# Sums of squares of the MLA latents moved behind the split transposes, and the first heads' weight splits moved to VectorE

## The chip, the cores and the metric

The kernel runs on one core of a Trainium2 chip. The metric is device time in microseconds (us). Engines are named as in the profile: PE is TensorE (PEld its weight loads), DVE is VectorE, ACT is ScalarE, POOL is GpSimd, SP is SyncE, whose queue issues the weight transfers.

## The reference, cut to what matters

Two blocks of two layers each run over 256 tokens of width 1024 in float32. The change lies in the first layer's mixer, an attention with low-rank latents (MLA):

```
proj = h @ w_in                    # 1024 -> 384 + 256 + 64
c_q, c_kv, k_pe = split(proj)
q  = rms_norm(c_q,  q_a_norm)  @ w_uq     # 8 heads x (128 + 64)
kv = rms_norm(c_kv, kv_a_norm) @ w_ukv    # 8 heads x (128 + 128)
k_pe = rope(rms_norm(k_pe, k_rope_norm))
```

Each `rms_norm` needs, per token, the sum of squares of its part: 384 columns of `c_q`, 256 of `c_kv`, 64 of `k_pe`. The attention of the eight heads, the output projection, an MLP and three more layers follow.

## The kernel before, in words

**Split products.** A float32 product is made of three matmuls on split operands: each operand is written as a rounded high part and a low part (the rest), and `mm3` (L174 to L176) issues high x high, high x low and low x high. So every weight and every activation is split once. `load_w` (L150 to L171) does it for weights: SP issues the transfer into a tile `raw` (L163), ACT writes `whi` (L166), and a second engine writes `wlo = raw - whi` (L167). That engine is VectorE unless the caller names others; `(G,)` names GpSimd. The tiles raw, whi and wlo are rings of four buffers each, 1024 columns wide: a transfer waits until the split four tiles earlier has been read, a split until the matmuls that read the tile four earlier are done. `evac_split` (L252 to L261) does it for activations that PE has transposed into PSUM: ACT writes the high part (L259), VectorE the low part (L260).

**The first mixer, `mla` (L482).** The input projection fills four PSUM banks, two for each of the two token tiles t: `a[t][0]` with the 384 columns of c_q, `a[t][1]` with the 256 of c_kv and the 64 of k_pe. These four are the whole ring `acc`. VectorE copies them to SBUF (`ct` and `kp`, L516 to L518). VectorE then takes the six sums of squares from these copies, with a multiply whose accumulator gives the sum (L519 to L522). PE transposes the latents, five blocks of 128 columns for both token tiles (L527), into the ring `aux` of four PSUM banks, and `evac_split` empties them into `cT`. The statistics `vv` (L535) and `rr` (a reciprocal square root by Newton steps on VectorE, L185 to L190) follow from the sums; the rotated `k_pe` follows from `rr`.

**Head pairs, `heads(hp)` (L561).** For each of four pairs of heads: the q weights (3 x 384 columns, in tiles of 768 and 384), nine `mm3` products' worth of matmuls for each token tile into `aq[t]`, then, for hp 0 and 2, the kv weights (two tiles of 1024 columns), and `ak[t]`. `aq[0]`, `aq[1]`, `ak[0]`, `ak[1]` take over the banks of `a[0][0]`, `a[0][1]`, `a[1][0]`, `a[1][1]`. ACT copies the results out (L579 to L582) and takes sums of squares; VectorE makes the head norms (L590, L595, L185 to L190, L600); PE transposes (L608); `attention(hp)` follows. For hp 0 alone both `load_w` calls name GpSimd.

**The order of the work.** The text gives priorities only. A planner lays the instructions of each engine in a queue by its own estimate of when each is ready, and the chip works off each queue in that order. So the second Newton step of `rr` stands, in the queue of VectorE, around the splits of the weights of pair 1. The planner runs anew for a changed text.

Of the kernel before, what the change touches and what calls it, by code (L numbers as in the profile page):

```python
# [13 lines left out]
AF = mybir.ActivationFunctionType  # L14
ALU = mybir.AluOpType
# [4 lines left out]
P = 128  # L20
S = 256
NT = 2
# [88 lines left out]
def kernel(ctx: ExitStack, tc: tile.TileContext, I: dict, out: bass.AP, small_at: dict):  # L111
    nc = tc.nc
    V, A, G, T = nc.vector, nc.scalar, nc.gpsimd, nc.tensor
# [10 lines left out]
    def slot(i, shape, dt=F32):  # L124

        return big.tile(shape, dt, tag=f"s{i}", name=f"s{i}")

    def w2k(shape, dt=F32):
        return wk.tile(shape, dt, tag="w2k", name="w2k", bufs=7)

    def w1k(shape, dt=F32):
        return wk.tile(shape, dt, tag="w1k", name="w1k", bufs=3)

    def acc_tile():
        return ps.tile([P, 512], F32, tag="acc", name="acc")

    def aux_tile():
        return ps.tile([P, 512], F32, tag="aux", name="aux")

    @contextmanager  # L140
    def queued(after):

        with ExitStack() as es:
            for i in after or ():
                es.enter_context(tc.issue_after(i))
            yield
# [3 lines left out]
    def load_w(src, a, b, engines=None, into=None, after=None):  # L150

        m = max(1, 1024 // b)
        parts = []
        for a0 in range(0, a, m):
            k = min(m, a - a0)
            raw = ring.tile([P, 1024], F32, tag="raw", name="raw")
            if into is None:
                hi = ring.tile([P, 1024], F32R, tag="whi", name="whi")
                lo = ring.tile([P, 1024], F32R, tag="wlo", name="wlo")
            else:  # L160
                hi, lo = (t[:, a0 * b:(a0 + k) * b] for t in into)
            rs = raw[:, :k * b]
            nc.sync.dma_start(rs.rearrange("p (a b) -> p a b", a=k), src[:, a0:a0 + k])  # L163
            e = V if engines is None else engines[a0 // m % len(engines)]
            with queued(after):
                i = A.activation(hi[:, :k * b], rs, AF.Copy)  # L166
                j = e.tensor_tensor(lo[:, :k * b], rs, hi[:, :k * b].bitcast(F32), op=ALU.subtract)  # L167
            split[:] = [i.ins, j.ins]
            for i in range(k):
                parts.append((hi[:, i * b:(i + 1) * b], lo[:, i * b:(i + 1) * b]))  # L170
        return parts  # L171
# [81 lines left out]
    def evac_split(hi, lo, p, g=None):  # L253

        if g is None:
            i = A.activation(hi, p, AF.Copy)
            j = V.tensor_tensor(lo, p, hi.bitcast(F32), op=ALU.subtract)
        else:
            i = A.activation(hi, p, AF.Copy, scale=g)  # L259
            j = V.scalar_tensor_tensor(lo, p, g, hi.bitcast(F32), op0=ALU.mult, op1=ALU.subtract)  # L260
        return i.ins, j.ins  # L261

    def pair_tile(i, n):
        return slot(i, [P, n, S], F32R), slot(i + 1, [P, n, S], F32R)
# [217 lines left out]
    def mla():  # L482
        hT = pair_tile(1, KD)
        w = wview("mla_w_in", 0)
        a = [[acc_tile() for _ in range(2)] for _ in range(NT)]
        grp = ((0, Q_RANK), (Q_RANK, KV_RANK + ROPE))
        behind = []
        for c in range(4):
            nc.sync.dma_start(xT0[:, 2 * c:2 * c + 2], I["xT"][:, 2 * c:2 * c + 2])
            for k in (2 * c, 2 * c + 1):  # L490
                hi = A.activation(hT[0][:, k], xT0[:, k], AF.Copy, scale=gain("attn_norm", k))
                lo = V.scalar_tensor_tensor(hT[1][:, k], xT0[:, k], gain("attn_norm", k), hT[0][:, k].bitcast(F32),
                                            op0=ALU.mult, op1=ALU.subtract)
            wc = load_w(w[:, 2 * c:2 * c + 2, :], 2, 704)
# [17 lines left out]
        ct = slot(13, [P, NT, 640])  # L512
        kp = w1k([P, NT, 1, ROPE])
        ss = st.tile([P, NT, 3], F32, tag="ss3", name="ss3")
        for t in range(NT):
            V.tensor_copy(ct[:, t, 0:384], a[t][0][:, 0:384])  # L516
            V.tensor_copy(ct[:, t, 384:640], a[t][1][:, 0:256])
            V.tensor_copy(kp[:, t, 0], a[t][1][:, 256:320])  # L518
        for t in range(NT):  # L519
            for j, (src, n) in enumerate(((ct[:, t, 0:384], 384), (ct[:, t, 384:640], 256), (kp[:, t, 0], 64))):  # L520
                jk = w2k([P, 512])
                V.scalar_tensor_tensor(jk[:, :n], src, 1.0, src, op0=ALU.mult, op1=ALU.mult, accum_out=ss[:, t, j:j + 1])  # L522
        cT = pair_tile(11, 5)
        for k in range(5):
            p = aux_tile()
            for t in range(NT):
                T.transpose(p[:, t * P:(t + 1) * P], ct[:, t, k * P:(k + 1) * P], ident)  # L527
            g = gain("mla_q_a_norm", k) if k < 3 else gain("mla_kv_a_norm", k - 3)
            evac_split(cT[0][:, k], cT[1][:, k], p[:, 0:256], g)
        vv = st.tile([P, NT, 3], F32, tag="vv", name="vv")  # L530
        rr = st.tile([P, NT, 3], F32, tag="rr", name="rr")
        ee = st.tile([P, NT], F32, tag="ee", name="ee")
# [20 lines left out]
        wq = wview("mla_w_uq", 0)  # L553
        wkv = wview("mla_w_ukv", 0)
# [4 lines left out]
        wkv_c, roped = [], []  # L559

        def heads(hp):  # L561
            wc = load_w(wq[:, :, hp * 384:(hp + 1) * 384], 3, 384, (G,) if hp == 0 else None)
            aq = [acc_tile() for _ in range(NT)]
            for t in range(NT):
                for k in range(3):
                    mm3(aq[t][:, :384], sl(cT, slice(None), k, slice(t * P, (t + 1) * P)), wc[k],
                        k == 0, k == 2)
            if hp % 2 == 0:
                wkv_c[:] = load_w(wkv[:, :, hp * 512:hp * 512 + 1024], 2, 1024, (G,) if hp == 0 else None)
            ak = [acc_tile() for _ in range(NT)]  # L570
            for t in range(NT):
                for k in range(2):
                    mm3(ak[t], sl(cT, slice(None), 3 + k, slice(t * P, (t + 1) * P)),
                        sl(wkv_c[k], slice(None), slice((hp % 2) * 512, (hp % 2) * 512 + 512)), k == 0, k == 1)
            s6 = st.tile([P, NT, 3, 2], F32, tag="s6", name="s6")
            r6 = st.tile([P, NT, 3, 2], F32, tag="r6", name="r6")
            raw = slot(9 + hp % 2, [P, NT, 2, 320])
            for t in range(NT):
                A.activation(raw[:, t, :, 0:192], aq[t][:, :384].rearrange("p (h d) -> p h d", h=2), AF.Copy)  # L579
                k3 = ak[t].rearrange("p (h d) -> p h d", h=2)  # L580
                A.activation(raw[:, t, :, 192:320], k3[:, :, 0:128], AF.Copy)
                A.activation(vt[:, t, 2 * hp:2 * hp + 2, :], k3[:, :, 128:256], AF.Copy, scale=rr[:, t, 1:2])  # L582
            for t in range(NT):
                for j in range(2):
                    for i, (src, n) in enumerate(((aq[t][:, 192 * j:192 * j + 128], P), (aq[t][:, 192 * j + 128:192 * j + 192], ROPE),
                                                  (ak[t][:, 256 * j:256 * j + 128], P))):
                        sq = w1k([P, P])
                        if i == 2:
                            rw = raw[:, t, j, (0, 128, 192)[i]:(0, 128, 192)[i] + n]
                            V.scalar_tensor_tensor(sq[:, 0:n], rw, 1.0, rw, op0=ALU.mult, op1=ALU.mult,  # L590
                                                   accum_out=s6[:, t, i, j:j + 1])
                        else:
                            A.activation(sq[:, 0:n], src, AF.Square, accum_out=s6[:, t, i, j:j + 1])
            f3 = lambda ap: ap.rearrange("p a b c -> p (a b c)")
            V.tensor_tensor(s6, s6, eq, op=ALU.add)  # L595
            rsqrt(f3(r6), f3(s6), 12)
            qn = w2k([P, NT, 2, P])
            kn = w2k([P, NT, 2, P])
            for dst, c0, i in ((qn, 0, 0), (kn, 192, 2)):
                V.tensor_tensor(dst, raw[:, :, :, c0:c0 + P], r6[:, :, i, :, None].to_broadcast([P, NT, 2, P]), op=ALU.mult)  # L600
            qr = w1k([P, NT, 2, ROPE])
            roped[:] = [rope_apply(G, qr, raw[:, :, :, 128:192], tabs["q"], 2)]
            V.tensor_tensor(qr, qr, r6[:, :, 1, :, None].to_broadcast([P, NT, 2, ROPE]), op=ALU.mult)
            for src, dst, g in ((qn, qT, gs[:, 0:1]), (kn, kT, gs[:, 3:4])):
                p = aux_tile()
                for j in range(2):
                    for t in range(NT):
                        T.transpose(p[:, j * S + t * P:j * S + (t + 1) * P], src[:, t, j], ident)  # L608
                A.activation(dst[:, 2 * hp:2 * hp + 2, :], p.rearrange("p (a b) -> p a b", a=2), AF.Copy, scale=g)
            p = aux_tile()  # L610
            for t in range(NT):
                T.transpose(p[:, t * P:(t + 1) * P], qr[:, t].rearrange("p a b -> p (a b)"), ident)
            V.tensor_copy(peT[:, hp, :], p[:, 0:256])
# [674 lines left out]
    with queued(mla()):  # L1288
        rel_bias_mask()
# [30 lines left out]
```

## Time and profile before

| | us |
|---|---|
| median of 3 runs | 964.49 |
| lowest, highest | 960.13, 966.01 |
| the profiled execution | 965.93 |
| its span, first to last instruction | 964.1 |
| mean granted clock of TensorE | 0.979 |

The span is what the rows below cover, counted from the first instruction; 1.8 us of the execution lie around it. An idle time of an engine is shown in brackets ahead of the instruction that ended it, with what released it. Instructions of one engine overlap a little at their ends: the distance from start to start is what one costs its queue.

### The profile page before, as it was taken

To read this page: it belongs to the slowest core of one execution; us is meant where nothing else is said; L and a number is where in the kernel's file an instruction comes from. 1 tells how busy PE (TensorE), PEld (TensorE's weight loads), DVE (VectorE), ACT (ScalarE), POOL (GpSimd) and SP (SyncE) were. 2 spreads that over 40 slices of the span, in tenths; PEclk is the share of its full clock that TensorE was granted. 3 is DMA by queue.
4 is the path that set the end of the run, shared out by engine and by line. 5 is a ranking of instruction groups with operands and counts; after the bars stand their busy time and mean duration, and the time that the engine had idled before them with its cause. 6 is when DMAs were issued, how large, how long until landed. Compare 5 with 4: busy or idle time off the path is not lost. (4 is left out here: it accounts for less than half of the span.)

```text
span 964.1 us, 14699 instructions
## 1 busy us (share of the span) xinstructions
PE 905.0 (94%) x5474; PEld 789.9 (82%) x5474; DVE 635.4 (66%) x1335; ACT 522.7 (54%) x967; POOL 151.1 (16%) x194
## 2 busy tenths in 40 slices
PE   8799889999999999999999999998995998998995
PEld 8676589989998878778999999888994986887784
DVE  6897376655556666757554555678983688757775
ACT  6576354644556556646534454478653136754652
POOL 1421122222222300022000000010387000000000
PEclk9799999999999999999999999999997999999998
DMA  8345247677767864436666566354843115445431
GB/s 292 115 146 186 66 131 220 192 198 214 205 197 209 166 196 151 154 109 198 196 195 198 175 195 183 105 166 140 215 149 98 45 41 181 135 170 174 133 109 67
DMA packets 97304, 154.62 MB, mean 160 GB/s; under 512 B 10840, under 2 KB 65920, under 8 KB 96976
## 3 DMA queue, kind: packets, MB, share of 16 engines
q1 hardware_dynamic: 87072, 141.53, 46.9%
q0 software_dynamic: 10016, 12.11, 6.0%
q8 instruction: 43, 0.70, 0.3%
q14 instruction: 29, 0.24, 0.1%
q10 hardware_dynamic: 144, 0.03, 0.0%
HBM read 147.84 MB, written 5.78 MB: 159 GB/s over the span
## 5 line engine op out<-in xcount | busy, mean ns | idle before, releaser
L167 DVE TENSOR_TENSOR wlo<-raw,whi 128x1024 fp32r<-128x1024 f32 (+3 forms) x194 | 236.7, 1223 | 201.9 <-ACT whi L166 200.6
L166 ACT ACTIVATE whi<-raw 128x1024 fp32r<-128x1024 f32 (+3 forms) x202 | 206.0, 1025 | 217.0 <-DMA raw<-in_mlp_w_in_dram 137.6
L174 PE MATMUL acc<-whi,s 128*128 128x512 f32 (+2 forms) x408 | 162.1, 401 | 3.5 <-ACT whi L166 2.6
L175 PE MATMUL acc<-wlo,s 128*128 128x512 f32 (+2 forms) x408 | 160.4, 394 | 0.5 <-DVE wlo L167 0.5
L176 PE MATMUL acc<-whi,s 128*128 128x512 f32 (+2 forms) x408 | 158.9, 391 | 0.0
L176 PE MATMUL aux<-s,wlo 128*128 128x256 f32 (+2 forms) x528 | 149.5, 283 | 3.1 <-DVE wlo L167 3.1
L174 PE MATMUL aux<-s,whi 128*128 128x256 f32 (+2 forms) x528 | 149.4, 283 | 2.3 <-DVE s L260 2.3
L175 PE MATMUL aux<-s,whi 128*128 128x256 f32 (+2 forms) x528 | 149.3, 283 | 0.0
L174 PEld LDWEIGHTS aux<-s,whi 128*128 128x128 f32 (+2 forms) x528 | 99.6, 189 | 4.6 <-DVE s L260 2.8
L176 PEld LDWEIGHTS aux<-s,wlo 128*128 128x128 f32 (+2 forms) x528 | 99.6, 189 | 3.9 <-DVE wlo L167 3.6
L174 PE MATMUL acc<-s,w2k 128*128 128x512 f32 x256 | 100.1, 391 | 1.7 <-ACT w2k L676 1.7
L176 PE MATMUL acc<-s,w2k 128*128 128x512 f32 x256 | 100.2, 391 | 1.1 <-DVE w2k L677 1.1
L175 PEld LDWEIGHTS aux<-s,whi 128*128 128x128 f32 (+2 forms) x528 | 99.6, 189 | 1.6
L175 PE MATMUL acc<-s,w2k 128*128 128x512 f32 x256 | 100.0, 391 | 0.0
L174 PEld LDWEIGHTS acc<-whi,s 128*128 128x128 f32 x408 | 77.6, 191 | 20.6 <-ACT whi L166 3.1
L176 PEld LDWEIGHTS acc<-whi,s 128*128 128x128 f32 x408 | 78.6, 193 | 14.0 <-DVE s L1278 0.3
L175 PEld LDWEIGHTS acc<-wlo,s 128*128 128x128 f32 x408 | 78.2, 192 | 13.2 <-DVE wlo L167 1.3
L167 DVE TENSOR_TENSOR s<-raw,s 128x1024 fp32r<-128x1024 f32 x64 | 75.7, 1219 | 5.3 <-ACT s L166 5.3
L176 PE MATMUL acc<-s,wlo 128*128 128x256 f32 x256 | 73.4, 288 | 6.2 <-DVE wlo L167 6.2
L175 PE MATMUL acc<-s,whi 128*128 128x256 f32 x256 | 73.7, 288 | 0.5 <-DVE s L260 0.2
L174 PE MATMUL acc<-s,whi 128*128 128x256 f32 x256 | 73.7, 288 | 0.4 <-ACT s L259 0.2
L166 ACT ACTIVATE s<-raw 128x1024 fp32r<-128x1024 f32 x68 | 68.3, 1048 | 7.2 <-DMA raw<-in_mlp_w_out_dram 6.0
(357 smaller groups left out, 1486.2 us busy)
## 6 DMA issues: line engine op xcount, KB each, us to landing
raw<-in_mlp_w_in_dram SPq DMA_DIRECT2D x64, 512.0 KB, 5.3
raw<-in_mlp_w_out_dram SPq DMA_DIRECT2D x64, 512.0 KB, 3.9
raw<-in_gdn_w_in_dram SPq DMA_DIRECT2D x32, 512.0 KB, 4.4
raw<-in_moba_w_qkv_dram SPq DMA_DIRECT2D x24, 512.0 KB, 4.4
raw<-in_fox_w_in_dram SPq DMA_DIRECT2D x16, 512.0 KB, 4.9
raw<-in_kv_w_dram SPq DMA_DIRECT2D x16, 512.0 KB, 3.9
raw<-in_mla_w_o_dram SPq DMA_DIRECT2D x8, 512.0 KB, 3.9
bias_d<-s POOLq DMA_DIRECT2D x64, 64.0 KB, 4.5
```

The costliest lines, as they stand in the source:

```text
L166: i = A.activation(hi[:, :k * b], rs, AF.Copy)
L167: j = e.tensor_tensor(lo[:, :k * b], rs, hi[:, :k * b].bitcast(F32), op=ALU.subtract)
L174: T.matmul(o, lhsT=l[0], rhs=r[0], start=start, stop=False)
L175: T.matmul(o, lhsT=l[0], rhs=r[1], start=False, stop=False)
L176: T.matmul(o, lhsT=l[1], rhs=r[0], start=False, stop=stop)
```

## The change

The sums of squares move, in the text, behind the transposes and their splits. The two sums of c_q (384 columns) go to ScalarE, from the copy in SBUF. The four sums of c_kv and k_pe stay on VectorE, but one of the two factors is read from PSUM, from `a[t][1]`, and the other from the copy. The two `load_w` calls of the first head pair no longer name GpSimd, so their four splits run on VectorE.

```diff
-        for t in range(NT):
-            for j, (src, n) in enumerate(((ct[:, t, 0:384], 384), (ct[:, t, 384:640], 256), (kp[:, t, 0], 64))):
-                jk = w2k([P, 512])
-                V.scalar_tensor_tensor(jk[:, :n], src, 1.0, src, op0=ALU.mult, op1=ALU.mult, accum_out=ss[:, t, j:j + 1])
         cT = pair_tile(11, 5)
         for k in range(5):
...
             evac_split(cT[0][:, k], cT[1][:, k], p[:, 0:256], g)
+        for t in range(NT):
+            jk = w2k([P, 512])
+            A.activation(jk[:, :384], ct[:, t, 0:384], AF.Square, accum_out=ss[:, t, 0:1])
+        for t in range(NT):
+            for j, (c0, n, src) in enumerate(((0, 256, ct[:, t, 384:640]), (256, 64, kp[:, t, 0]))):
+                jk = w2k([P, 512])
+                V.scalar_tensor_tensor(jk[:, :n], a[t][1][:, c0:c0 + n], 1.0, src, op0=ALU.mult, op1=ALU.mult,
+                                       accum_out=ss[:, t, 1 + j:2 + j])
...
-            wc = load_w(wq[:, :, hp * 384:(hp + 1) * 384], 3, 384, (G,) if hp == 0 else None)
+            wc = load_w(wq[:, :, hp * 384:(hp + 1) * 384], 3, 384)
...
-                wkv_c[:] = load_w(wkv[:, :, hp * 512:hp * 512 + 1024], 2, 1024, (G,) if hp == 0 else None)
+                wkv_c[:] = load_w(wkv[:, :, hp * 512:hp * 512 + 1024], 2, 1024)
```

## Rows read from the trace of the kernel before

**Rows 1.** The page, part 1: PE's busy time and share.

```profile
PE 905.0 (94%) x5474; PEld 789.9 (82%) x5474; DVE 635.4 (66%) x1335; ACT 522.7 (54%) x967; POOL 151.1 (16%) x194
```

**Rows 2.** Busy time by stretch (start:end and length first; PEclk is the granted clock).

```profile
core 0: us, PE busy (x) PEld busy (x) DVE busy (x) ACT busy (x) POOL busy (x), PEclk, DMA share, GB/s
...
28.00:34.00 6.00, 0.69 (x2) 0.38 (x3) 6.00 (x10) 1.17 (x2) 4.96 (x2) 0.59 0.53 159
34.00:39.00 5.00, 5.00 (x17) 5.00 (x17) 2.94 (x19) 1.81 (x3) 0.00 (x0) 0.50 0.15 39
...
50.00:92.00 42.00, 41.10 (x207) 30.57 (x208) 37.38 (x120) 28.73 (x92) 9.63 (x13) 1.00 0.58 182
```

**Rows 3.** Waits of PE from 22 to 50 us: total, times, longest.

```profile
PE aux L527 <- DVE s L260: 5.0, 1, 5.0
PE acc L174 <- ACT whi L166: 1.0, 1, 1.0
```

**Rows 4.** VectorE in order of time: start, duration, line, operation, [idle before].

```profile
25.61 0.21 DVE L518 COPY w1k<-acc 128x64 f32<-128x64 f32 x1
25.75 1.06 DVE L522 SCALAR_TENSOR_TENSOR w2k<-s 128x384 f32<-128x384 f32 x1
...
27.88 0.22 DVE L522 SCALAR_TENSOR_TENSOR w2k<-w1k 128x64 f32<-128x64 f32 x1
...
28.51 2.56 DVE L522 SCALAR_TENSOR_TENSOR w2k<-s 128x256 f32<-128x256 f32 x1
...
31.00 2.35 DVE L522 SCALAR_TENSOR_TENSOR w2k<-w1k 128x64 f32<-128x64 f32 x1
...
33.27 2.25 DVE L260 SCALAR_TENSOR_TENSOR s<-aux,gains,s 128x256 fp32r<-128x256 f32 x5
35.44 0.29 DVE L535 SCALAR_TENSOR_TENSOR vv<-ss,ee 128x2 f32<-128x2 f32 x3
```

**Rows 5.** GpSimd in order of time: the first head pair's splits.

```profile
24.57 3.10 POOL L167 TENSOR_TENSOR wlo<-raw,whi 128x768 fp32r<-128x768 f32 x2 [1.44 <-ACT whi L166]
28.30 4.96 POOL L167 TENSOR_TENSOR wlo<-raw,whi 128x1024 fp32r<-128x1024 f32 x2 [0.63 <-ACT whi L166]
```

**Rows 6.** PE in order of time, around its wait and behind it.

```profile
26.73 0.34 PE L174 MATMUL acc<-whi,s 128*128 128x384 f32 x1
26.90 0.33 PE L175 MATMUL acc<-wlo,s 128*128 128x384 f32 x1
...
33.80 0.69 PE L527 MATMUL aux<-gains,s 128*128 128x128 f32 x2 [5.03 <-DVE s L260]
34.15 0.67 PE L176 MATMUL acc<-whi,s 128*128 128x384 f32 x1
...
38.77 0.63 PE L175 MATMUL acc<-wlo,s 128*128 128x512 f32 x1
...
41.58 0.41 PE L174 MATMUL acc<-whi,s 128*128 128x384 f32 x1
```

**Rows 7.** VectorE behind the statistics: splits for pair 1, pair 0's norm, pair 2's split.

```profile
38.98 0.96 DVE L167 TENSOR_TENSOR wlo<-raw,whi 128x768 fp32r<-128x768 f32 x1 [1.78 <-ACT whi L166]
...
39.95 0.56 DVE L167 TENSOR_TENSOR wlo<-raw,whi 128x384 fp32r<-128x384 f32 x1
...
49.49 1.29 DVE L600 TENSOR_TENSOR w2k<-s,r 128x512 f32<-128x512 f32 x2
...
51.25 1.22 DVE L167 TENSOR_TENSOR wlo<-raw,whi 128x1024 fp32r<-128x1024 f32 x1
```

**Rows 8.** ScalarE in order of time: a sum of squares, the latents' high parts, weight splits.

```profile
21.27 0.62 ACT L240 ACTIVATE w2k<-x 128x512 f32<-128x512 f32 x1
...
25.71 1.57 ACT L259 ACTIVATE s<-aux,gains 128x256 fp32r<-128x256 f32 x4 [0.69 <-PE aux L527]
27.15 2.02 ACT L166 ACTIVATE whi<-raw 128x1024 fp32r<-128x1024 f32 x2
...
38.10 0.84 ACT L166 ACTIVATE whi<-raw 128x768 fp32r<-128x768 f32 x1 [0.84 <-PE acc L176]
```

## The prediction

> **What bounds the kernel now.** I read the page first: PE is busy 94% of the span [rows 1], so what can be won is where PE stands still or runs slowly. The busy time by stretch shows the one such place near the change. [...] The waits name the cause: PE stands 5.0 us at the fifth transpose of the latents, because all four aux banks wait for VectorE's low parts (L260), and 1.0 us before that for a weight's high part [rows 3].
>
> VectorE's own order then says why L260 is late. The copies end at 25.75. Six sums of squares follow and last until 33.27, when the five low parts begin together; the statistics begin at 35.44 [rows 4]. A sum over 64 columns takes 0.22 us at 27.88, and the same operation takes 2.35 us at 31.00; 256 columns take 2.56 [rows 4]. The long ones lie exactly beside GpSimd's two splits of 1024 columns, 28.20 to 33.26, and the short ones in GpSimd's pause ahead of them [rows 5]: VectorE, with both factors in SBUF, waits out GpSimd's instruction. So the sums stretch from what would be two to three microseconds to 7.5, and PE, the latents and the clock pay.
>
> Behind the stall both engines are dense: from 50 to 92 us PE is busy 41.1 and VectorE 37.4 of 42 [rows 2]. Whatever is won in front should therefore reach the end as a shift, but VectorE is the second bound, close behind PE. That decides the size.
>
> **The change part by part.** I follow VectorE's queue from the end of the copies (25.75) to the first head pair's norm (L600 at 49.49 [rows 7]), since the attention of the first heads starts from there.
>
> *Removed.* The six sums: 33.27 - 25.75 = 7.52 us of VectorE [rows 4]. On GpSimd 3.10 + 4.96 = 8.06 us go [rows 5]; it has nothing to do in this stretch, so this is worth nothing by itself.
>
> *Added on VectorE: four sums with one factor in PSUM.* The trace of before has no such sum. From below stand the five low parts, which read PSUM and SBUF at 256 columns, 2.25 / 5 = 0.45 each, and 0.22 for 64 columns; from above the stretched 2.56 and 2.35 [rows 4]. The upper ends need GpSimd at work, and with its splits gone nothing of it is left here, so I take the lower: 2 x (0.45 + 0.22) = 1.34 us. At the upper ends it would be 9.8, and the change would lose 8.5 on this term.
>
> [...]
>
> *Added on VectorE: four splits.* 768 columns 0.96, 384 columns 0.56, 1024 columns 1.22 each [rows 7]; they overlap at the ends by about 0.08, so 0.88 + 0.48 + 2 x 1.14 = 3.64 us. That they cost VectorE nothing, because they fit into gaps, is the lower end; 3.96 is the upper.
>
> *Added on ScalarE: two squares of 384 columns.* One of 512 takes 0.62 [rows 8]; with the reading of the accumulator I put 0.6 each, 1.2 in all. ScalarE works on the high parts until 29.17 [rows 8] and is busy only 1.17 us from 28 to 34 [rows 2], so behind these they are hidden. If the planner puts them in front, the high parts and the kv weights' splits come 1.2 us later.
>
> *A stall that goes on VectorE.* The split of pair 1 at 38.98 stands between two Newton steps and makes VectorE wait 1.78 us for ScalarE's high part [rows 7], which itself waited for PE to finish pair 0's q matmuls, whose tile it takes over [rows 8]. PE finishes these earlier, so I count the 1.78 as won; the lower end is 0.
>
> *Sum on VectorE:* 7.52 - 1.34 - 3.64 + 1.78 = 4.3 us.
>
> *PE by itself.* The stall of 5.0 and the wait of 1.0 go [rows 3]. From 34.15 to 38.77 fourteen matmuls of 384 columns ran at the low clock, 0.33 us each; at the high level the step is 0.17 (26.73 to 26.90) [rows 6], so 4.62 - 14 x 0.17 = 2.2 us. Together 8.2: what PE alone could give.
>
> *New waits, and what is late next.* In the new order VectorE ends its copies at 25.75, takes sums (1.3), low parts (2.2) and splits (3.6) in some order, and is through at about 32.9. PE's q products need the latents and the splits of 768 and 384, so they run in part from about 27 and end near 31 to 32; the kv products need the two splits of 1024, whose high parts exist at 28.2 and 29.2 [rows 8], and end near 35 instead of 41.58 [rows 6]. Late next are thus VectorE's splits for kv, then the statistics and norms on VectorE. `aq[1]` and `ak[1]` now wait for the sums, since these hold the banks of `a[t][1]`; behind them in PE's order stand the other q products. With sums of 0.45 this is cheaper than the splits that PE waits for anyway, so I cost it at nothing; with the sums last in VectorE's order it would hold PE until about 33, still before 33.80. On SP's queue the q weights of pair 1 wait for the raw buffers, now freed by VectorE and not by GpSimd; these tiles are needed only after pair 0's q products, so nothing is added.
>
> So PE is offered 8.2 us, VectorE can follow by 4.3 until L600. As the two engines are coupled by every head, I take VectorE's 4.3. The profiled execution goes from 965.93 to 961.6. It lies 1.4 us above the median of the runs shown, so against the median I forecast 964.49 - 4.3 = **960.2 us**.
>
> **The rivals.**
>
> *PE's full gap.* Splits for later pairs may step aside in VectorE's queue, and the Newton steps leave small gaps that splits can fill. Then PE's 8.2 us count: 956.3. For it speaks that PE is the denser engine from 50 to 92 [rows 2]; against it that VectorE carries 3.64 us more splits just ahead of the norms.
>
> *Given back.* Without the 1.78 us, and with the shift partly lost where the planner weaves heads and projections anew, the gain is 7.52 - 1.34 - 3.96 = 2.2 less what is lost behind: 0 to 2 us, 962.5 to 964.5. For it speaks that the queue order is planned anew; against it that the work behind the stage is the same.
>
> *Slower: the kv splits ahead of the latents.* The planner may believe the kv weights ready early and put their two splits ahead of the latents' low parts, and the squares ahead of the high parts. Then VectorE stands until ScalarE has written the second kv high part, 29.17 + 1.2 = 30.4, splits it until 31.6, and ends the low parts at 33.8, the very time at which PE resumed before [rows 6]. All 18 q matmuls of pair 0 then run at the low clock, 18 x 0.33 = 5.9, until 39.7; before, the first four were done and the rest ended at about 38.1 [rows 6, 8]. The split of pair 1 comes 1.6 us later, and VectorE with it: 964.49 + 1.6 = 966.1. It decides from the point where a split of 1024 columns stands ahead of L260 on VectorE. For it speaks that before the change PE already met a kv weight 1.0 us too early [rows 3]; against it that the latents stand ahead in the text.
>
> *The stall only moves.* If the sums stay ahead of the low parts, since they are ready first, the change does only half of what it says; but without GpSimd they cost 1.34 there and not 7.52. That is inside the forecast.
>
> **How the numbers follow.** Forecast (gain of 2.2 to 6.5) 0.55; PE's full gap, with some luck of the planner beyond it, 0.22; given back 0.13; slower by 1.6, or by another order elsewhere, 0.10. About 1% (9.6 us) is what a measurement of this kernel tells from no change; 8.2 lies under it, so only the part of the second case with luck behind the mixer passes it: 0.10. Slower by over 1% needs a new order that costs much elsewhere: 0.03. The rest, 0.87, is within 1%. The forecast's own range is 958.0 to 962.3. The range for 8 in 10 takes in PE's full gap and the slower case, with one more microsecond at each end for the spread of the runs: 955.0 to 966.5.
>
> **What would show it.** In the changed profile: the five L260 begin by 27 us and not at 33.27; no sum of squares on VectorE over 0.6 us; no L167 on GpSimd before 40; PE's wait at L527 under 1 us, and the clock at the higher level from 34 to 39; L535 by 33; L600 of pair 0 at about 45 instead of 49.49, and the same shift at 92 us. I am wrong in size if L600 comes at 42 (PE decides) or at 48 (VectorE is fuller than I think), and wrong in mechanism if PE still stands over 3 us between 26 and 34, or if L600 comes early and the end does not.

## The result, and the profile after

Twenty runs of each kernel: median 961.68 us after, 967.42 us before, ratio 0.9936 with a 95% interval of 0.9918 to 0.9953. By the ratio that is 6.2 us less (4.5 to 7.9; the two medians lie 5.7 apart), where 4.3 were forecast: the sign came out, and the change stays within 1%; the size is a third to a half more. That the time itself, forecast as 960.2, was missed by only 1.5 us is in part luck: the three runs the forecast started from (median 964.49) lie 2.9 us below the median of all twenty, and the gain by the medians was 1.4 us larger than forecast, so the two errors partly cancel. The two profiled executions have spans of 964.1 and 957.0 us.

PE's busy time is what it was [rows 1]; the span around it became shorter (the page's line of the engines):

```profile
PE 904.7 (95%) x5474; PEld 787.2 (82%) x5474; DVE 630.7 (66%) x1335; ACT 524.3 (55%) x971; POOL 144.3 (15%) x190
```

The busy time by stretch of the changed kernel, with the columns of rows 2:

```profile
28.00:34.00 6.00, 5.38 (x22) 3.42 (x20) 6.00 (x25) 4.68 (x9) 0.00 (x0) 1.00 0.49 149
34.00:39.00 5.00, 3.31 (x20) 3.09 (x20) 4.30 (x24) 3.92 (x24) 0.66 (x2) 1.00 0.84 231
...
50.00:92.00 42.00, 39.64 (x194) 29.18 (x193) 34.99 (x114) 27.76 (x87) 7.81 (x11) 0.97 0.55 173
```

From 28 to 34 us PE works 5.38 us where it worked 0.69, and the granted clock is 1.00 in both stretches where it was 0.59 and 0.50 [rows 2]; GpSimd is silent and VectorE as full as before. VectorE in order of time shows what it does instead:

```profile
25.25 0.21 DVE L518 COPY w1k<-acc 128x64 f32<-128x64 f32 x1
25.38 0.95 DVE L167 TENSOR_TENSOR wlo<-raw,whi 128x768 fp32r<-128x768 f32 x1
26.24 2.06 DVE L260 SCALAR_TENSOR_TENSOR s<-aux,gains,s 128x256 fp32r<-128x256 f32 x5
28.22 0.41 DVE L532 SCALAR_TENSOR_TENSOR w2k<-acc,s 128x256 f32<-128x256 f32 x1
...
28.55 0.22 DVE L532 SCALAR_TENSOR_TENSOR w2k<-acc,w1k 128x64 f32<-128x64 f32 x1
...
29.19 0.30 DVE L539 SCALAR_TENSOR_TENSOR vv<-ss,ee 128x2 f32<-128x2 f32 x3
...
30.23 1.22 DVE L167 TENSOR_TENSOR wlo<-raw,whi 128x1024 fp32r<-128x1024 f32 x1
31.36 0.16 DVE L188 SCALAR_TENSOR_TENSOR rs_b<-rr,vv 128x6 f32<-128x6 f32 x1
31.44 1.22 DVE L167 TENSOR_TENSOR wlo<-raw,whi 128x1024 fp32r<-128x1024 f32 x1
...
43.69 1.29 DVE L604 TENSOR_TENSOR w2k<-s,r 128x512 f32<-128x512 f32 x2
```

The five low parts begin at 26.24 and not at 33.27 [rows 4]. Four sums follow, 0.97 us from 28.22 to 29.19, and the statistics begin at 29.19 instead of 35.44. The planner put the first weight split (768 columns) ahead of the low parts and wove the others between the Newton steps. The first pair's norm (now L604) comes at 43.69 instead of 49.49 [rows 7], 5.8 us earlier. PE in order of time, its waits in brackets:

```profile
26.84 0.38 PE L523 MATMUL aux<-gains,s 128*128 128x128 f32 x2
...
30.30 0.44 PE L175 MATMUL acc<-wlo,s 128*128 128x384 f32 x1 [0.37 <-DVE wlo L167]
...
31.50 0.50 PE L175 MATMUL acc<-wlo,s 128*128 128x512 f32 x1 [0.25 <-DVE wlo L167]
...
35.78 0.45 PE L174 MATMUL acc<-whi,s 128*128 128x384 f32 x1 [1.69 <-ACT s L586]
```

The stall of 5.03 us at the fifth transpose [rows 6] is gone. What is late next is a wait of 1.69 us for ScalarE's copy of the values, which needs `rr`, whose Newton steps VectorE now interrupts for weight splits.

The 5.8 us hold until 90 us. PE's products for two attention outputs there read, in the kernel before and then after the change:

```profile
95.12 0.49 PE L360 MATMUL aux<-w2k,s 128*128 128x128 f32 x2 [0.64 <-ACT w2k L358]
...
102.68 0.49 PE L360 MATMUL aux<-w2k,s 128*128 128x128 f32 x2 [1.31 <-ACT w2k L358]
```

```profile
89.30 0.58 PE L360 MATMUL aux<-w2k,s 128*128 128x128 f32 x2 [0.64 <-ACT w2k L358]
98.39 0.49 PE L360 MATMUL aux<-w2k,s 128*128 128x128 f32 x2 [1.31 <-ACT w2k L358]
```

The same waits stand in front, but the lead shrinks from 5.82 to 4.29 us: from 89.6 to 93.0 the granted clock of this execution was 0.50; in the execution of before it was 1.00 there, and 1.00 again from 95.4 to 99.0. In a second profile of each kernel the first of these products stands at 92.92 and 89.33, a lead of 3.6 us: what the change gains in this stage is read as 5.8 from one pair of profiles and as 3.6 from the other.

### The profile page after: what moved, and what is told of

The parts are those of the page before. It is cut to its first block, busy times and chain, and to the rows that moved or that the text cites. A ratio compares the mean times of both kernels' runs of the same rounds, so it can differ in the third digit from the quotient of the medians.

```text
span 957.0 us, 14701 instructions
## 1 busy us (share of the span) xinstructions
PE 904.7 (95%) x5474; PEld 787.2 (82%) x5474; DVE 630.7 (66%) x1335; ACT 524.3 (55%) x971; POOL 144.3 (15%) x190
## 5 line engine op out<-in xcount | busy, mean ns | idle before, releaser
L167 DVE TENSOR_TENSOR wlo<-raw,whi 128x1024 fp32r<-128x1024 f32 (+3 forms) x198 | 239.5, 1213 | 198.9 <-ACT whi L166 197.5
L174 PEld LDWEIGHTS acc<-whi,s 128*128 128x128 f32 x408 | 76.5, 189 | 23.0 <-ACT whi L166 3.8
L176 PEld LDWEIGHTS acc<-whi,s 128*128 128x128 f32 x408 | 76.9, 189 | 13.9 <-issue 0.3
L167 DVE TENSOR_TENSOR s<-raw,s 128x1024 fp32r<-128x1024 f32 x64 | 75.7, 1219 | 6.1 <-ACT s L166 6.1
```

Source lines behind the costliest of these rows:

```text
L174: T.matmul(o, lhsT=l[0], rhs=r[0], start=start, stop=False)
L176: T.matmul(o, lhsT=l[1], rhs=r[0], start=False, stop=stop)
```

## The experiments

I use two measures. The *stretch* is the time on VectorE from the end of the copies to the first pair's norm: 49.49 - 25.75 = 23.74 us before, 43.69 - 25.38 = 18.31 after. It is read from one profile and leaves out the rest of the kernel. The ratio is that of the whole time to the kernel before, which ran beside each kernel on the same chip; the chips differ from run to run.

Three things differ between the kernels: the place of the sums in the text (early, ahead of the transposes, or late, behind the splits), their form (old: all on VectorE, both factors from SBUF; new: two on ScalarE, four with a factor in PSUM), and who makes the first pair's splits (GpSimd or VectorE).

| sums' place, form | splits | copies end | norm | stretch | ratio (95%) |
|---|---|---|---|---|---|
| early, old (before) | GpSimd | 25.75 | 49.49 | 23.74 | 1 |
| the same again | GpSimd | 25.98 | 47.30 | 21.32 | 1.0003 (0.9977 to 1.0029) |
| late, old | GpSimd | 25.68 | 45.97 | 20.29 | 0.9945 (0.9920 to 0.9969) |
| early, new | GpSimd | 25.30 | 45.57 | 20.27 | 0.9956 (0.9926 to 0.9985) |
| late, new | GpSimd | 25.94 | 48.22 | 22.28 | 0.9947 (0.9924 to 0.9969) |
| early, old | VectorE | 25.03 | 46.13 | 21.10 | 0.9980 (0.9957 to 1.0003) |
| late, old | VectorE | 25.14 | 46.38 | 21.24 | 0.9985 (0.9962 to 1.0008) |
| early, new | VectorE | 24.92 | 44.44 | 19.52 | 0.9922 (0.9896 to 0.9948) |
| late, new (after) | VectorE | 25.38 | 43.69 | 18.31 | 0.9936 (0.9918 to 0.9953) |
| the same again | VectorE | 25.41 | 43.72 | 18.31 | 0.9911 (0.9880 to 0.9943) |

The two measures do not rank the parts alike. By the ratio, every change to the sums that keeps GpSimd (0.9945, 0.9956, 0.9947) cannot be told from the whole change (0.9936), while the splits' move with the old sums (0.9980, 0.9985) can be told from it and not from no change. So the time shows a gain from the sums, and does not show that moving the splits adds to it; what the splits' move does is read from the stretches alone, and with GpSimd in it a stretch changes by up to 2.4 us from one profile of a kernel to the next (23.74 and 21.32).

**Only the splits move to VectorE (early, old).**

```diff
-load_w(wq[...], 3, 384, (G,) if hp == 0 else None)
+load_w(wq[...], 3, 384)
-load_w(wkv[...], 2, 1024, (G,) if hp == 0 else None)
+load_w(wkv[...], 2, 1024)
```

> Only the splits move to VectorE; all six sums stay on VectorE, from SBUF, ahead of the low parts. Measured is the stretch on VectorE from the end of the copies to the first head pair's norm: 23.74 us before, 18.31 after the change. Contention theory (a sum with both factors in SBUF waits out GpSimd's split): without GpSimd the six sums cost about 2.0 us and not 7.52, no sum over 0.6 us, stretch 19 to 20, and 4 us or more of the gain is there, 0.4% faster. Order theory (what costs is that the sums stand ahead of the low parts): no gain, stretch above 22.5. Slow-GpSimd theory (only the late low parts of the weights count): gain as in the full change.

VectorE of this kernel:

```profile
25.50 0.42 DVE L522 SCALAR_TENSOR_TENSOR w2k<-s 128x256 f32<-128x256 f32 x1
...
25.85 0.22 DVE L522 SCALAR_TENSOR_TENSOR w2k<-w1k 128x64 f32<-128x64 f32 x1
...
46.13 1.29 DVE L600 TENSOR_TENSOR w2k<-s,r 128x512 f32<-128x512 f32 x2
```

PE of this kernel:

```profile
30.81 0.69 PE L175 MATMUL acc<-wlo,s 128*128 128x384 f32 x1 [2.28 <-DVE wlo L167]
```

With GpSimd silent the same operations take 0.42 and 0.22 us instead of up to 2.56 and 2.35, and all six sums 1.93 (25.03 to 26.96). The contention is real. But the stretch is 21.10, not 19 to 20, hardly less than in the second profile of the kernel before (21.32), and the time is not told from that of before. PE now stands 2.28 us for the split of 768 columns, which VectorE makes only behind the statistics.

**Only place and form of the sums change (late, new, GpSimd).** The sums as in the change; both `load_w` calls keep `(G,)`.

> Only the sums move and change their source (ScalarE, or one factor in PSUM); the four splits of the first pair stay on GpSimd. Contention theory: sums with one factor in PSUM do not wait for GpSimd, 0.2 to 0.45 us each; VectorE is 3.6 us lighter than after the change, but the kv products wait for GpSimd's second split, near 33 us; stretch 16 to 18.5, as fast as the full change or 1 us faster. Slow-GpSimd theory: no gain, since the kv splits end at 33 as before; stretch above 22. If the PSUM factor does not protect, sums of 2 us and more show, and the stretch is 20 to 22.

VectorE of this kernel, then GpSimd:

```profile
29.43 0.41 DVE L532 SCALAR_TENSOR_TENSOR w2k<-acc,s 128x256 f32<-128x256 f32 x1
...
30.40 2.96 DVE L539 SCALAR_TENSOR_TENSOR vv<-ss,ee 128x2 f32<-128x2 f32 x3
33.28 2.41 DVE L555 TENSOR_SCALAR eq<-vv 128x4 f32<-128x4 f32 x2
```

```profile
29.99 5.68 POOL L167 TENSOR_TENSOR wlo<-raw,whi 128x384 fp32r<-128x384 f32 x3 [2.22 <-DVE w2k L532]
```

The sums with a factor in PSUM take 0.41 and 0.22, as expected. The stretch is 22.28, not 16 to 18.5. GpSimd's split of 384 columns itself began late: the profile puts its wait down to a sum on VectorE, of which the split needs nothing, but its high part stands on ScalarE only at 29.40, behind the second of the squares that moved there (28.89). And the waiting went on to the next operations of VectorE, the statistics: three instructions over two columns, with both inputs in SBUF, took 2.96 us, against 0.29 [rows 4]. The two `eq` operations behind them, over four columns and with a single input from SBUF, took 2.41, against 0.24 at 29.40 after the change: two inputs in SBUF are not the only case that waits. The time fell by 0.5% nonetheless (0.3 to 0.8), more than this one profile explains; that stays open.

**Only the place of the sums changes (late, old, GpSimd).**

```diff
+        # behind evac_split, unchanged:
         for t in range(NT):
             for j, (src, n) in enumerate(...):
                 V.scalar_tensor_tensor(jk[:, :n], src, 1.0, src, ...)
```

> Only the place in the text moves: all six sums on VectorE from SBUF, behind the low parts, splits on GpSimd. Contention theory: the sums now fall beside GpSimd's two splits of 1024 columns and still take 4 to 6 us in sum, so the statistics begin at 33 or later; PE's stall at the fifth transpose goes; stretch 20 to 22.5, a third to a half of the gain. Order theory: stretch 18 to 19, all of the gain.

VectorE of this kernel in order of time:

```profile
28.33 2.40 DVE L529 SCALAR_TENSOR_TENSOR w2k<-w1k 128x64 f32<-128x64 f32 x1
...
31.07 2.33 DVE L529 SCALAR_TENSOR_TENSOR w2k<-s 128x384 f32<-128x384 f32 x1
...
45.97 1.29 DVE L600 TENSOR_TENSOR w2k<-s,r 128x512 f32<-128x512 f32 x2
```

PE of this kernel:

```profile
38.07 0.44 PE L174 MATMUL acc<-whi,s 128*128 128x384 f32 x1 [3.17 <-ACT s L582]
```

As the contention theory said, two sums meet the splits again, at 2.40 and 2.33 us, beside GpSimd's two splits of 1024 columns (4.75 us from 28.24). The stretch is 20.29, the lower edge of what was expected by it: PE no longer stands at the fifth transpose. It stands 3.17 us later instead, for ScalarE's copy, which needs `rr` and so the late sums. Measured by the whole time, the order theory (all of the gain) is not excluded: 0.9945 (0.9920 to 0.9969) cannot be told from the change.

**Place and splits, old form (late, old, VectorE).**

> Place and splits as in the change, but all six sums on VectorE from SBUF. With GpSimd silent each sum costs its bare price (0.5, 0.35 and 0.2 us), 2.0 in all against 0.97 with the ScalarE and PSUM form: stretch 19 to 19.6, about 1 us behind the full change, not to be told from it in the time. If the source mattered by itself, the stretch would be above 20.

PE of this kernel:

```profile
30.90 0.63 PE L175 MATMUL acc<-wlo,s 128*128 128x384 f32 x1 [2.48 <-DVE wlo L167]
```

A miss: 21.24 instead of 19 to 19.6. The planner again put the split of 768 columns behind the statistics, and PE waits 2.48 us. A sum of the old form (25.14) stands where that split stands after the change (25.38); whether that is the planner's reason is not shown. So neither of my two theories was complete. The next two kernels ask whether it is the place of that split or the sums' form.

**Early, new, VectorE.**

> The changed kernel with the sums back at their old place in the text, ahead of the transposes; sources and splits as in the change. In this kernel's queue VectorE takes the sums first, then the low parts, and the first weight split (768 columns) only behind the statistics; after the change that split stands ahead of the low parts. Place theory (PE's first q products starve for that split, stand over 2 us and drop the clock, as in the two runs with the splits on VectorE and the sums from SBUF): PE waits about 2 us for L167, stretch 20 to 20.8 against 18.31. Source theory (the sums' form alone makes the difference between 21.1 and 18.3): stretch 18.2 to 18.8.

PE of this kernel:

```profile
28.57 1.22 PE L174 MATMUL acc<-whi,s 128*128 128x512 f32 x2 [1.71 <-ACT whi L166]
```

19.52, between the two expectations: the place costs 1.2 us of stretch. PE stood 1.71 us, but at a high part of the kv weights, not at L167. In time it cannot be told from the change.

**The first q weights loaded earlier in the text (late, old, VectorE).**

```diff
+        wq = wview("mla_w_uq", 0)
+        wc0 = load_w(wq[:, :, 0:384], 3, 384)      # ahead of the copies
-            wc = load_w(wq[:, :, hp * 384:(hp + 1) * 384], 3, 384)
+            wc = wc0 if hp == 0 else load_w(wq[:, :, hp * 384:(hp + 1) * 384], 3, 384)
```

> As the run with all six sums from SBUF behind the transposes and the splits on VectorE, but the load of the first q weights stands in the text ahead of the copies, so both their splits come ahead of the low parts in VectorE's queue; nothing else differs. Place theory: PE's wait of 2.48 us for L167 goes, the stretch falls from 21.24 to 19 to 19.6 although the sums cost their 2.0 us. Source theory: stretch stays at 20.8 to 21.5.

VectorE of this kernel:

```profile
24.90 1.42 DVE L167 TENSOR_TENSOR wlo<-raw,whi 128x768 fp32r<-128x768 f32 x2
...
44.84 1.29 DVE L602 TENSOR_TENSOR w2k<-s,r 128x512 f32<-128x512 f32 x2
```

The splits of 768 and 384 columns now stand at 24.90, and one copy (0.13 us) behind them; counted from 25.03 the stretch is 19.81, against 21.24 with the text otherwise the same. The place theory gave 19 to 19.6: right but for 0.2. The ratio goes from 0.9985 to 0.9944 (0.9918 to 0.9971); the two intervals overlap. What the sums' form is worth at equal places is read against the same hoist in the changed kernel (18.85, the first of the two attempts below): 19.81 - 18.85 = 0.96, just the difference of the sums' bare prices (1.93 against 0.97). So of the 2.9 us between the old and the new form (21.24 to 18.31), 1.4 are the place of both q splits, 1.0 the sums' form, and 0.5 that after the change only the split of 768 columns stands ahead of the low parts.

**The kernel before, again.**

> The kernel before, unchanged, against itself: what the spread of a profile and of five rounds is. Expected: ratio within 0.0025 of 1; stretch 23.7 within 0.5, with one sum over 256 and one over 64 columns above 2 us again. If the stretch moves by more than 1 us, the meeting of the sums and GpSimd's splits is chance and single profiles decide less.

VectorE in this second profile, then GpSimd and PE:

```profile
28.51 0.41 DVE L522 SCALAR_TENSOR_TENSOR w2k<-s 128x256 f32<-128x256 f32 x1
...
28.85 2.35 DVE L522 SCALAR_TENSOR_TENSOR w2k<-w1k 128x64 f32<-128x64 f32 x1
...
47.30 1.29 DVE L600 TENSOR_TENSOR w2k<-s,r 128x512 f32<-128x512 f32 x2
```

```profile
28.54 4.91 POOL L167 TENSOR_TENSOR wlo<-raw,whi 128x1024 fp32r<-128x1024 f32 x2 [0.87 <-ACT whi L166]
```

```profile
31.67 0.69 PE L527 MATMUL aux<-gains,s 128*128 128x128 f32 x2 [2.66 <-DVE s L260]
```

The ratio is 1.0003, but the stretch 21.32 and not 23.74: one sum waited out a split of 1024 columns here, two did in the first profile, and PE's stall at the fifth transpose is 2.66 us and not 5.03. The sum that starts at 28.51, just ahead of GpSimd's split at 28.54, slips through in 0.41 us; the one that starts at 28.85, behind it, takes 2.35. What I read as the price of the contention is a draw.

**The change, again.**

> The changed kernel once more: what of its gain stays in a second profile and five rounds. Expected: ratio 0.992 to 0.9955; stretch 18.3 within 0.4, since no sum meets GpSimd any more and nothing in it is chance; TensorE's clock from 8.5 to 12 us at the higher level, as in all six kernels without GpSimd's splits so far (at the lower one in all four with them). If the stretch moves by over 1 us, the 5.4 us of the first pair of profiles is no measure of the change.

VectorE in this second profile of the changed kernel:

```profile
25.41 0.95 DVE L167 TENSOR_TENSOR wlo<-raw,whi 128x768 fp32r<-128x768 f32 x1
...
43.72 1.29 DVE L604 TENSOR_TENSOR w2k<-s,r 128x512 f32<-128x512 f32 x2
```

The stretch is 18.31 to the hundredth: with GpSimd's splits out of it, it came out the same in both profiles. The ratio 0.9911 (0.9880 to 0.9943) overlaps the first one.

**Only the form of the sums changes (early, new, GpSimd).**

> The last of the eight combinations: only the sums' form changes (ScalarE, one factor in PSUM), at the old place, splits on GpSimd. Contention theory: no sum over 0.5 us, the low parts start by 26.5, and the stall at the fifth transpose goes; then PE waits for GpSimd's kv splits until 33 to 35; stretch 20 to 22.3, ratio 0.994 to 0.998. If the clock at the start goes with GpSimd's splits, it is at the lower level from 8.5 to 12 us and the copies end at 25.7 to 26.0, not at 24.9 to 25.4.

VectorE of this kernel, then GpSimd:

```profile
25.30 0.41 DVE L525 SCALAR_TENSOR_TENSOR w2k<-acc,s 128x256 f32<-128x256 f32 x1
...
29.88 2.23 DVE L188 SCALAR_TENSOR_TENSOR rs_b<-rr,vv 128x6 f32<-128x6 f32 x1
32.15 2.29 DVE L189 TENSOR_TENSOR rs_b<-rs_b,rr 128x6 f32<-128x6 f32 x1
```

```profile
25.29 1.82 POOL L167 TENSOR_TENSOR wlo<-raw,whi 128x768 fp32r<-128x768 f32 x1 [1.94 <-DVE s L517]
...
29.72 4.71 POOL L167 TENSOR_TENSOR wlo<-raw,whi 128x1024 fp32r<-128x1024 f32 x2 [1.04 <-DVE eq L555]
```

This shows both halves side by side. At 25.30 the sum with one factor in PSUM runs at its bare 0.41 us beside GpSimd's split; at 29.88 and 32.15 two Newton steps over six columns, both inputs in SBUF, take 2.23 and 2.29 us instead of 0.17, one for each split of 1024. The stretch, 20.27, and the ratio came as expected; the guess on the end of the copies did not (25.30).

**Two attempts to go further.** First, the q weights' load hoisted as above, in the changed kernel:

> The changed kernel with the load of the first q weights ahead of the copies in the text, so that the split of 384 columns too stands ahead of the low parts. Place theory taken further: PE's wait of 0.37 us for that split goes, but the low parts end 0.5 us later; stretch 18.0 to 18.6, time as the change within the interval. If the place of this split were worth as much as that of 768 columns was (1.4 us), stretch 17.

VectorE of this kernel:

```profile
25.20 1.42 DVE L167 TENSOR_TENSOR wlo<-raw,whi 128x768 fp32r<-128x768 f32 x2
...
44.18 1.29 DVE L606 TENSOR_TENSOR w2k<-s,r 128x512 f32<-128x512 f32 x2
```

44.18 - 25.33 = 18.85, above the 18.0 to 18.6 expected and half a microsecond longer than after the change, about the price of the split of 384 columns now ahead of the low parts. The ratio is 0.9958 (0.9933 to 0.9984), not faster.

Second, the wait that is late next, PE for ScalarE's scaled copy:

```diff
+                if hp == 0:
+                    A.activation(v2, k3[:, :, 128:256], AF.Copy)
+                    G.tensor_scalar(v2, v2, rr[:, t, 1:2], None, op0=ALU.mult)
+                else:
-                A.activation(vt[...], k3[:, :, 128:256], AF.Copy, scale=rr[:, t, 1:2])
+                    A.activation(v2, k3[:, :, 128:256], AF.Copy, scale=rr[:, t, 1:2])
```

> The changed kernel, and for the first pair ScalarE copies the values out without their factor rr, and GpSimd multiplies them in place later. What is late next after the change, by its profile: PE waits 1.69 us for ScalarE's copy L586, which waits for rr. If that wait holds the chain: PE's wait goes, ScalarE's squares of pair 0 begin before 35.3 instead of 36.3, stretch 17.0 to 17.6, about 1 us or 0.1% faster than the change, too little for the time to tell. If VectorE itself is full: stretch 18.1 to 18.6 and PE waits elsewhere.

VectorE of this kernel, then PE:

```profile
38.36 0.96 DVE L167 TENSOR_TENSOR wlo<-raw,whi 128x768 fp32r<-128x768 f32 x1 [0.41 <-ACT whi L166]
...
43.46 1.22 DVE L167 TENSOR_TENSOR wlo<-raw,whi 128x1024 fp32r<-128x1024 f32 x1
45.30 1.29 DVE L609 TENSOR_TENSOR w2k<-s,r 128x512 f32<-128x512 f32 x2
```

```profile
34.15 0.44 PE L174 MATMUL acc<-whi,s 128*128 128x384 f32 x1 [0.28 <-ACT s L588]
```

A miss on both expectations: PE's wait fell from 1.69 to 0.28 us, but the stretch rose to 20.16. The planner put a split of 1024 columns (43.46) ahead of the first pair's norm, which after the change stands behind it; why it did is not shown. The ratio is 0.9963 (0.9939 to 0.9987). Neither version beats the change.

## Why the prediction was right, and where its size was off

*What bounds the kernel.* Right. The sums beside GpSimd's splits, the low parts behind them and PE's stall at the fifth transpose were the loss, and what is won there is carried on by two dense engines (5.8 us at the first pair's norm, 49.49 to 43.69, and still 5.82 at 95.12).

*The signs named.* Low parts by 27 (26.24), no sum on VectorE over 0.6 (0.42 at most), no split on GpSimd before 40, no wait at the transposes, the higher clock from 34 to 39 (1.00), statistics by 33 (29.19): all came. The norm was put at about 45 and came at 43.69.

*Sum on VectorE*, the step that failed, in size: 7.52 - 1.34 - 3.64 + 1.78 = 4.3 against 23.74 - 18.31 = 5.4 measured. Its terms: the sums cost 0.97 and not 1.34 (0.4 too much: 0.22 and 0.41 were the durations, but the next instruction starts 0.15 and 0.34 behind). The five low parts take 1.98 where they took 2.17 (0.2, not counted). The remaining 0.5 is that splits between dependent Newton steps fill the waits from step to step: after the change the distance from one step to the next is 0.20 us where nothing stands between (34.25 to 34.45), and a split begins 0.08 after a step's start (31.36 to 31.44). From the first statistic to the first use of `rr`, less the splits in between and the 1.78, VectorE takes 2.46 us before (35.44 to 41.02) and 1.99 after (29.19 to 35.25). I had named this under *PE's full gap* and counted it at nothing. The splits themselves were right (0.86 + 0.47 + 2 x 1.13 = 3.6), as was the 1.78.

*The sums behind GpSimd, 7.52 us.* Right for that one execution, but a second one of the same kernel has 31.14 - 25.98 = 5.16, so that the size of this term was in part luck. (GpSimd's splits of 1024 columns began at 28.30 [rows 5]; the prediction has 28.20. It changes no sum.) By that pair the stretch shrinks by 3.0 and not 5.4 us. The measured 6.2 (4.5 to 7.9) covers the larger, not the smaller; the earlier end of the copies, 0.4 to 0.6 us, is the same in both pairs. That profiles alone add up to the measured time is not shown.

*The factor in PSUM.* The prediction put these sums at the 0.45 and 0.22 us that it read from before [rows 4], with nothing on top for the source. The traces agree: 0.41 us at 256 columns with a factor in PSUM (after the change) against 0.42 without (the splits alone moved), 0.22 against 0.22 at 64. Beside GpSimd's split of 768 columns the four sums ran at the same 0.41 and 0.42, 0.22 and 0.22 (early, new, GpSimd, from 25.30). With both factors in SBUF a sum of 256 columns took 1.22 beside the split of 384 (before, at 26.74) and 2.56 beside one of 1024 [rows 4]; three instructions over two columns from SBUF took 2.96 for 0.29 (late, new, GpSimd), two Newton steps 2.23 and 2.29 for 0.17 (early, new, GpSimd). A split of 1024 took GpSimd 2.48 us before (4.96 / 2 [rows 5]) and 2.36 in that last kernel (4.71 / 2), so a single operation that waited, at 2.56, 2.23 or 2.29, took about as long as one such split. The two `eq` operations with one input waited as well (2.41 us in all); what decides which operations wait is not shown. The sum of 256 columns beside the split of 384, in the kernel before:

```profile
26.74 1.22 DVE L522 SCALAR_TENSOR_TENSOR w2k<-s 128x256 f32<-128x256 f32 x1
```

*New waits.* The sums' hold on the banks of `a[t][1]` cost nothing, as said. ScalarE's squares were hidden after the change, though the planner put them ahead (23.95 and 26.79), where the prediction had feared 1.2 us: the low parts run from 26.24 without a gap. What was late next was named one step too early: not the kv splits (0.25 us) but `rr` (1.69).

*The rivals.* The slower order, with the kv splits ahead of the low parts, did not come; the planner put one q split there. (Its price of 1.6 us compared 39.7 with 38.1; by rows 6 the q products ended at 38.8, which leaves 0.9.) "The stall only moves" asked for the sums ahead of the low parts, and they stand behind them; the kernel that has that order (early, new, VectorE) gains all the same, as the prediction said. A stall did move in each half alone: with the sums' form changed and GpSimd kept, the wait went to Newton steps and statistics; with only their place changed, it stayed on the sums, and PE stood for `rr`; with only the splits moved, PE stood for L167. *PE's full gap*, 8.2 us, lies outside the interval of the twenty runs (4.5 to 7.9) and inside that of the second measurement, 8.6 (5.5 to 11.6); it is not settled.

## What to carry to other kernels

Help from GpSimd was not free here: beside its splits of 1024 columns (2.36 us each) two of VectorE's Newton steps, six columns with both inputs in SBUF, took 2.23 and 2.29 us instead of 0.17, so look for short operations that take as long as GpSimd's. With one victim taken away the wait moved to the next, from the sums to the statistics (2.96 us; late, new, GpSimd) or to the Newton steps (2.23 and 2.29; early, new, GpSimd). The shortest stretch, 18.31, had the long GpSimd instructions out of it and the sums with one input from PSUM, which kept their 0.41 and 0.22 us beside GpSimd too. Where two instructions meet by a few hundredths of a microsecond, as at 28.51 and 28.54, take a second profile before you price the meeting. When a planner orders the queues, ask of every edit what it lets into the gap: here 1.4 us of the stretch hung on whether the first q splits stood ahead of the latents' low parts or behind the statistics.

## What was not expected

The clock in the start-up goes with the first pair's splits, which run 15 us later. From 8.5 to 12 us the granted clock was 0.52 to 0.64 in all five profiles with these splits on GpSimd, and 1.00 in all eight without. Before and after, the busy time of that stretch:

```profile
8.50:12.00 3.50, 3.41 (x11) 3.41 (x12) 3.47 (x13) 2.66 (x5) 0.00 (x0) 0.52 0.92 303
```

```profile
8.50:12.00 3.50, 3.50 (x24) 3.48 (x23) 3.46 (x12) 2.50 (x5) 0.44 (x1) 1.00 0.95 304
```

Before, PE began its first products at 7.47 us, after at 6.97; by the end of the copies, 25.75 and 25.38, the lead is 0.4 us, so little of it is left for what follows. What makes PE begin earlier, and whether the clock follows from that, was not tried and is open.

Short stretches at the lower clock come and go with the execution: one around 90 us (0.50 from 89.6 to 93.0) cost the changed kernel 1.5 us of its lead in its profile; the kernel before had none there in its first profile (1.00 from 88 to 104) and one in its second (0.71 from 90 to 100). So a gain of 5 us is read from the stretch where it is made, in more than one profile, and not from the ends of two spans.
